# The first mixer's width-31 convolution as three of half the length, and a new order of the stage around it

## The chip, the core and the metric

The kernel runs on one core of a Trainium2 chip. The metric is the time of one execution on the device in microseconds (us), the median of several runs. PE is the matrix engine (TensorE), DVE the vector engine, ACT the scalar engine, POOL the GpSimd engine, SP the queue engine that issues most DMAs.

## What is computed

Four residual layers on 1024 frames of 1024 channels: a pool-and-convolution mixer, a gated FFN, a spatial gating unit and a second gated FFN, each behind an RMS norm. The change is in the first mixer alone:

```python
def pool_conv_mixer(h, w_in, pool_w, pool_scale, conv_w, conv_b, cn_g, cn_b, w_out):
    z = h @ w_in
    za = z[..., :D_POOL]
    zb_val = z[..., D_POOL:D_POOL + D_CONV]
    zb_gate = z[..., D_POOL + D_CONV:]
    pa = multiscale_pool_residual(za.reshape(bsz, s, POOL_GROUPS, POOL_GW))   # windows 2, 4, 8, 16: trailing mean minus za
    ya = jnp.einsum("bsgc,gcd->bsgd", pa, pool_w).reshape(bsz, s, D_POOL) * pool_scale
    gl = zb_val * jax.nn.sigmoid(zb_gate)
    yb = jax.nn.silu(layer_norm(causal_dwconv(gl, conv_w, conv_b), cn_g, cn_b))   # 31 taps per channel
    return jnp.concatenate([ya, yb], axis=-1) @ w_out
```

`D_POOL` and `D_CONV` are 512 each, so that there are four pool groups and four convolution blocks of 128 channels.

## The kernel before

Channels lie on the 128 partitions, frames along the free dimension, in two halves `h` of 512 frames (`HS`). Every fp32 product is made as three fp32r products of high and low parts (`mm3`, L185 to L189): a weight tile is loaded, ACT casts it to its high part `H` (L169), POOL subtracts to get the low part `L` (L170), and PE does H·H, H·L and L·H. A `gemm` of one 128-channel output block and both halves is 48 products of 512 columns. Weight tiles pass through few buffers (two raw, four for high and low parts), so a tile's cast waits for PE's last use of an earlier one.

The stage `mix0` runs, in PE's order: the value and gate of convolution block 0 (`gemm_pair`), with the norm of half 1 woven in (`n0`: the sums `st_n`, the root `r_n` on POOL, the broadcast `bc_n`; `have_rb` then makes `rb` and the first `glu`); value and gate of block 1; and then in turn the projections `za` of the four pool groups and the values and gates of blocks 2 and 3. Each `glu` makes `gl` = value × sigmoid(gate) in SBUF, with the norm's factor `rb` taken in (DVE L876 and L879, ACT L877, and L878 on POOL for blocks 1 to 3).

The convolution doesn't use PE. `conv(c, h, acc)` makes one half of one block: ACT starts `pc` in PSUM with one tap (L797), DVE adds taps one by one with a multiply-add over 512 frames (L807), and `NSIDE[c]` of the 31 taps go another way: ACT scales into `pr` (L801) and POOL adds (L805). DVE joins both sums (L812). The two halves of a block take turns (`convs`).

A pool group takes `u` from PSUM (DVE L899), forms its windowed sums by doubling on POOL (`s`, L904), and ends in `pa` on POOL (L911), once for each half. PE then mixes the group's channels (`ppool`, L916), and ACT and DVE split the result into `yaH` and `yaL` (L921, L922).

Behind that come `out_ya` (PE `poa`, 384 products), in which the layer norm `ln(0)` is woven (means `mb` of the four convolution outputs L936, sums `st_ln`, broadcast `bc_ln`, swish), then `out_yb` for each half (`pob`, 96 products each), with `ln(1)` in the first, and then the first FFN (`qa_u`).

PE's order is fixed by the program: it is the order of the code, with `later(n, fn)` hanging a step into a list that `tick` runs down by the count of 512-column products. The delays are the tables `LN0`, `LN1` and `N0LAG` and the arguments of `pool_group(g, delay)`. The other engines' orders are set when the program is built, by a scheduler that estimates when each instruction could start; the instructions of one engine then run in that order, each waiting for what it reads.

Of the kernel before, what the change touches and what calls it, by code (L numbers as in the profile page):

```python
# [10 lines left out]
F32 = mybir.dt.float32  # L11
# [3 lines left out]
ALU = mybir.AluOpType  # L15
# [13 lines left out]
PAD = 32  # L29

NSIDE = (9, 6, 8, 12)
# [4 lines left out]
LEAD = 6  # L36

LN0 = (36, 10, 4)
LN1 = (8, 10, 5)
WARM = 9  # L40
N0LAG = (20, 33)
# [28 lines left out]
def trunk_kernel(ctx: ExitStack, tc: tile.TileContext, a: dict, out: bass.AP):  # L70
# [708 lines left out]
    with stage("mix0", 8) as mp:  # L779
        pw = mp.tile([P, 4, P], F32, name="pw")  # L780
        gl = [mp.tile([P, PAD + S], F32, name=f"gl{c}") for c in range(4)]
        for c in range(4):
            nc.gpsimd.memset(gl[c][:, :PAD], 0.0)
        y = [[None, None] for _ in range(4)]

        def conv(c, h, acc):


            def src(k):
                o = PAD + h * HS - (CW - 1 - k)  # L790
                return gl[c][:, o : o + HS]

            def w(k):
                return col("conv_w", c * CW + k)

            n = f"{c}{h}"
            nc.scalar.activation(acc, src(CW - 1), AF.Identity, bias=col("conv_b", c), scale=w(CW - 1))  # L797
            side = None
            for k in range(NSIDE[c]):
                pr = mp.tile([P, HS], F32, tag="pr" if k else "side", name=f"pr{n}_{k}", bufs=2)  # L800
                nc.scalar.activation(pr, src(k), AF.Copy, scale=w(k))  # L801
                if side is None:
                    side = pr
                else:
                    nc.gpsimd.tensor_tensor(side, side, pr, op=ALU.add)  # L805
            for k in range(CW - 2, NSIDE[c] - 1, -1):
                yield nc.vector.scalar_tensor_tensor(acc, src(k), w(k), acc, op0=ALU.mult, op1=ALU.add)  # L807
            if h == 0:
                y[c][0] = mp.tile([P, HS], F32, tag="y", name=f"y{c}0", bufs=4)
            else:  # L810
                y[c][1] = gl[c][:, PAD + HS :]
            nc.vector.tensor_tensor(y[c][h], acc, side, op=ALU.add)  # L812

        def convs(a_, b_, lead=0):

            runs = [conv(*i, ps("pc%d%d" % i)) for i in (a_, b_)]
            for step in range(lead):
                ins = next(runs[0])
            with tc.issue_after(ins.ins) if lead else nullcontext():
                while runs:  # L820
                    runs = [r for r in runs if next(r, None) is not None]
# [384 lines left out]
```

## Time and profile before

| | us |
|---|---|
| median of 3 runs (1885.22 to 1887.01) | 1886.92 |
| the profiled execution | 1887.98 |
| its span in the trace | 1885.6 |
| from the start to the end of the last pool mix | 163.9 |
| from there to the first product of the first FFN (at 287.13) | 123.2 |

The granted clock of PE was 0.988 over the span. Times in the rows are microseconds from the start of the span unless marked ns. PE's matmuls are pipelined: a row's duration holds the modelled end of the last of them, and the step from one start to the next is what a product takes from the stream.

### The profile page before, as it was taken

Reading aid. Unit: us, or ns where it says so; the run is one execution under the profiler, and the core shown is the slowest. Engines: PE = TensorE matmul, PEld = TensorE weight load, DVE = VectorE, ACT = ScalarE, POOL = GpSimd, SP = SyncE. Lnnn points to the kernel's source line nnn. Section 1 sums busy time; section 2 is a strip of 40 time slices with the busy share of each in tenths; the row PEclk is TensorE's granted clock in tenths of the full one; section 3 lists DMA queues with packets and bytes.
Section 4 is the critical chain, followed back from the end, with each engine's and each line's share of the span. In section 5 each row is a group of like instructions: output and inputs, shape, how many; then the busy total and the mean of one; then the engine's idle time right before and its main releaser. Section 6 shows DMA issues by size and latency. Waiting matters only on the chain. (4 is left out here: it accounts for less than half of the span.)

```text
span 1885.6 us, 22755 instructions
## 1 busy us (share of the span) xinstructions
PE 1829.3 (97%) x8088; PEld 1501.4 (80%) x8092; DVE 1269.2 (67%) x1672; ACT 930.3 (49%) x1684; POOL 1238.9 (66%) x902
## 2 busy tenths in 40 slices
PE   8999888999999999999899999999999999999997
PEld 6787667888888888888778888777888888888886
DVE  5899788567676766886620247575767676768874
ACT  6436454655555565444431233356555555653461
POOL 2899667877777765685432445678777777656851
PEclk8999989999999999999999999999999999999998
DMA  4111121345444456542111222303444445565412
GB/s 157 45 46 34 54 92 34 115 131 168 145 146 156 149 175 233 185 134 79 43 48 56 90 89 101 100 23 123 155 147 163 150 146 167 168 234 167 141 56 89
DMA packets 113984, 223.26 MB, mean 118 GB/s; under 512 B 8784, under 2 KB 54864, under 8 KB 113872
## 3 DMA queue, kind: packets, MB, share of 16 engines
q1 hardware_dynamic: 113584, 221.55, 35.8%
q8 instruction: 63, 1.03, 0.2%
q14 instruction: 49, 0.40, 0.1%
q10 hardware_dynamic: 288, 0.28, 0.0%
HBM read 171.46 MB, written 50.33 MB: 118 GB/s over the span
## 5 line engine op out<-in xcount | busy, mean ns | idle before, releaser
L630 POOL TENSOR_TENSOR w<-d,w 128x512 fp32r<-128x512 f32 x154 | 232.1, 1527 | 124.0 <-ACT w L672 123.9
L357 POOL TENSOR_TENSOR w_u<-S_u,w_u 128x512 fp32r<-128x512 f32 x160 | 208.4, 1302 | 113.5 <-ACT w_u L356 113.5
L334 PE MATMUL p<-set,w 128*128 128x512 f32 x616 | 240.8, 391 | 3.6 <-DVE set L323 3.6
L333 PE MATMUL p<-set,w 128*128 128x512 f32 x616 | 240.9, 391 | 0.6 <-ACT set L322 0.6
L335 PE MATMUL p<-set,w 128*128 128x512 f32 x616 | 240.2, 390 | 0.0
L357 POOL TENSOR_TENSOR w_u<-r_u,w_u 128x512 fp32r<-128x512 f32 x120 | 156.6, 1305 | 59.5 <-ACT w_u L356 58.5
L333 PE MATMUL qb_u<-set,w_u 128*128 128x512 f32 x480 | 187.0, 389 | 0.1
L334 PE MATMUL qb_u<-set,w_u 128*128 128x512 f32 x480 | 186.7, 389 | 0.0
L335 PE MATMUL qb_u<-set,w_u 128*128 128x512 f32 x480 | 186.7, 389 | 0.0
L322 ACT CAST set<-hid 128x512 fp32r<-128x512 f32 x154 | 90.8, 620 | 162.6 <-DVE hid L630 97.4
L323 DVE TENSOR_TENSOR set<-hid,set 128x512 fp32r<-128x512 f32 x132 | 129.9, 1015 | 55.3 <-ACT set L322 52.9
L559 DVE SCALAR_TENSOR_TENSOR z<-qb_u,cols,z 128x511 f32<-128x511 f32 x88 | 65.9, 749 | 140.6 <-ACT z L557 139.1
L356 ACT CAST w_u<-S_u 128x512 fp32r<-128x512 f32 x160 | 98.7, 617 | 93.8 <-PE qb_u L335 60.8
L334 PEld LDWEIGHTS p<-set,w 128*128 128x128 f32 x616 | 116.0, 188 | 29.3 <-DVE set L323 5.3
L333 PEld LDWEIGHTS p<-set,w 128*128 128x128 f32 x616 | 115.9, 188 | 25.3 <-ACT set L322 1.0
L335 PEld LDWEIGHTS p<-set,w 128*128 128x128 f32 x616 | 116.1, 188 | 23.8
L335 PE MATMUL qa_u<-set,w_u 128*128 128x512 f32 x320 | 124.6, 389 | 0.6 <-POOL w_u L357 0.6
L333 PE MATMUL qa_u<-set,w_u 128*128 128x512 f32 x320 | 124.6, 389 | 0.2 <-ACT w_u L356 0.2
L334 PE MATMUL qa_u<-set,w_u 128*128 128x512 f32 x320 | 124.5, 389 | 0.0
L333 PE MATMUL qe_u<-set,w_u 128*128 128x512 f32 x320 | 124.5, 389 | 0.0
L334 PE MATMUL qe_u<-set,w_u 128*128 128x512 f32 x320 | 124.5, 389 | 0.0
L335 PE MATMUL qe_u<-set,w_u 128*128 128x512 f32 x320 | 124.5, 389 | 0.0
(241 smaller groups left out, 4772.0 us busy)
## 6 DMA issues: line engine op xcount, KB each, us to landing
r_u<-in_w_up SPq DMA_DIRECT2D x88, 512.0 KB, 3.4
hid<-z SPq DMA_DIRECT2D x44, 512.0 KB, 3.1
ws<-in_w_down SPq DMA_DIRECT2D x88, 256.0 KB, 3.6
sums<-ws SPq DMA_DIRECT2D x88, 256.0 KB, 3.7
hid<-hid SPq DMA_DIRECT2D x44, 512.0 KB, 5.6
d<-sums SPq DMA_DIRECT2D x40, 512.0 KB, 4.3
d<-in_w_down SPq DMA_DIRECT2D x30, 512.0 KB, 4.0
r_wv<-in_od_in SPq DMA_DIRECT2D x16, 512.0 KB, 3.8
```

The lines of the kernel that those rows point to most:

```text
L322: nc.scalar.copy(t[:, 0], src)
L323: leng.tensor_tensor(t[:, 1], src, t[:, 0].bitcast(F32), op=ALU.subtract)
L333: nc.tensor.matmul(o, H, xH, start=first, stop=False, skip_group_check=True)
L334: nc.tensor.matmul(o, H, xL, start=False, stop=False, skip_group_check=True)
L335: nc.tensor.matmul(o, L, xH, start=False, stop=last, skip_group_check=True)
L356: nc.scalar.copy(H, src)
L357: nc.gpsimd.tensor_tensor(L, src, H.bitcast(F32), op=ALU.subtract)
L559: nc.vector.scalar_tensor_tensor(o[:, s:], src[:, : HS - s], w[2 - s], o[:, s:], op0=ALU.mult, op1=ALU.add)
L630: eng.tensor_tensor(o, one, two, op=op)
```

## The change

- A block's convolution is split by even and odd frames. `gl` is stored de-interleaved, `xe` and `xo` of 512 each behind a pad of 16 (`CT`), and POOL adds `xs` = `xe` + `xo` over 528 elements, from both halves of the frames at once. Three convolutions of length 512 follow: `e` of `xe` with the 16 even taps, `o` of `xo` with the 15 odd ones, and one of `xs` with the 16 sums of neighbouring taps. Even outputs are `e` plus `o` shifted by one, odd ones are the third minus `e` and `o`. Results are written over `gl` with a step of two elements.
- Per block there are then 45 or 46 taps over 512 elements where there were 62. `NSIDE` of the 16 summed taps go by ACT and POOL: (9, 9, 11, 14), once per block, where (9, 6, 8, 12) went there for each half. `tap_sums` makes the summed taps and twice the bias on DVE, right behind the load of `cols`.
- `glu` reads its PSUM operands and `rb` with a step of two and writes de-interleaved.
- `val_gate(3)` stands ahead of `conv(2)` and the pool groups 1 and 0, and `conv(3)` ahead of `pool_group(0)`. The lead of the last convolution (`LEAD`, `convs`) goes.
- `ln(1)` is hung in before `out_ya`, with a delay of 54 products in place of 8 behind it. The norm's lags become 42 (from 33) and 7 (from 3). The buffers of `rb` are their own.

```diff
@@ -26,19 +26,18 @@
 DFF = 2816
 NF = DFF // P
 NB = 2
-PAD = 32
-
-NSIDE = (9, 6, 8, 12)
+
+CT = (CW + 1) // 2
+
+NSIDE = (9, 9, 11, 14)
 
 BUFS = {"wr": 2, "wh": 4}
 FFN_BUFS = {"hl": 4, "raw": 2, "z": 3}
 
-LEAD = 6
-
 LN0 = (36, 10, 4)
-LN1 = (8, 10, 5)
+LN1 = (54, 10, 5)
 WARM = 9
-N0LAG = (20, 33)
+N0LAG = (20, 42)
 NORM_LAG = ((8, 10), (6, 5))
 
 SUM_TWICE = (4, 8, 12, 16)
@@ -778,52 +777,76 @@
 
     with stage("mix0", 8) as mp:
         pw = mp.tile([P, 4, P], F32, name="pw")
-        gl = [mp.tile([P, PAD + S], F32, name=f"gl{c}") for c in range(4)]
+
+        gl_flat = [mp.tile([P, 2 * CT + S], F32, name=f"gl{c}") for c in range(4)]
+        gl = [g.rearrange("p (r n) -> p r n", r=2) for g in gl_flat]
         for c in range(4):
-            nc.gpsimd.memset(gl[c][:, :PAD], 0.0)
-        y = [[None, None] for _ in range(4)]
-
-        def conv(c, h, acc):
-
-
-            def src(k):
-                o = PAD + h * HS - (CW - 1 - k)
-                return gl[c][:, o : o + HS]
+            nc.gpsimd.memset(gl[c][:, :, :CT], 0.0)
+        y = [[g[:, 2 * CT + h * HS : 2 * CT + (h + 1) * HS] for h in range(2)] for g in gl_flat]
+        wsum = mp.tile([P, 4, CT], F32, name="wsum")
+        bias2 = mp.tile([P, 4], F32, name="bias2")
+
+        def tap_sums():
+
+            c0 = COLS["conv_w"]
+            w = cols[:, c0 : c0 + 4 * CW].rearrange("p (c k) -> p c k", k=CW)
+            nc.vector.tensor_copy(wsum[:, :, :1], w[:, :, :1])
+            nc.vector.tensor_tensor(wsum[:, :, 1:], w[:, :, 1::2], w[:, :, 2::2], op=ALU.add)
+            b0 = COLS["conv_b"]
+            nc.vector.tensor_tensor(bias2, cols[:, b0 : b0 + 4], cols[:, b0 : b0 + 4], op=ALU.add)
+
+
+
+
+
+        def conv(c):
+            xe, xo = [gl[c][:, r] for r in range(2)]
+            xs = mp.tile([P, CT + HS], F32, tag="xs", name=f"xs{c}", bufs=2)
+            nc.gpsimd.tensor_tensor(xs, xe, xo, op=ALU.add)
+            b = col("conv_b", c)
 
             def w(k):
                 return col("conv_w", c * CW + k)
 
-            n = f"{c}{h}"
-            nc.scalar.activation(acc, src(CW - 1), AF.Identity, bias=col("conv_b", c), scale=w(CW - 1))
+            def late(src, d):
+                return src[:, CT - d : CT - d + HS]
+
+            e, o = [ps(f"pc{i}{c}") for i in "eo"]
+            nc.scalar.activation(e, late(xe, 0), AF.Identity, bias=b, scale=w(CW - 1))
+            nc.scalar.activation(o, late(xo, 0), AF.Copy, scale=w(CW - 2))
             side = None
             for k in range(NSIDE[c]):
-                pr = mp.tile([P, HS], F32, tag="pr" if k else "side", name=f"pr{n}_{k}", bufs=2)
-                nc.scalar.activation(pr, src(k), AF.Copy, scale=w(k))
+                pr = mp.tile([P, HS], F32, tag="pr" if k else "side", name=f"pr{c}_{k}", bufs=2)
+                ws = wsum[:, c, k : k + 1]
                 if side is None:
+                    nc.scalar.activation(pr, late(xs, CT - 1 - k), AF.Identity, bias=bias2[:, c : c + 1], scale=ws)
                     side = pr
                 else:
+                    nc.scalar.activation(pr, late(xs, CT - 1 - k), AF.Copy, scale=ws)
                     nc.gpsimd.tensor_tensor(side, side, pr, op=ALU.add)
-            for k in range(CW - 2, NSIDE[c] - 1, -1):
-                yield nc.vector.scalar_tensor_tensor(acc, src(k), w(k), acc, op0=ALU.mult, op1=ALU.add)
-            if h == 0:
-                y[c][0] = mp.tile([P, HS], F32, tag="y", name=f"y{c}0", bufs=4)
-            else:
-                y[c][1] = gl[c][:, PAD + HS :]
-            nc.vector.tensor_tensor(y[c][h], acc, side, op=ALU.add)
-
-        def convs(a_, b_, lead=0):
-
-            runs = [conv(*i, ps("pc%d%d" % i)) for i in (a_, b_)]
-            for step in range(lead):
-                ins = next(runs[0])
-            with tc.issue_after(ins.ins) if lead else nullcontext():
-                while runs:
-                    runs = [r for r in runs if next(r, None) is not None]
+
+            def add(acc, src, d, wt):
+                nc.vector.scalar_tensor_tensor(acc, late(src, d), wt, acc, op0=ALU.mult, op1=ALU.add)
+
+            for d in range(1, CT):
+                add(e, xe, d, w(CW - 1 - 2 * d))
+                if d < CT - 1:
+                    add(o, xo, d, w(CW - 2 - 2 * d))
+            yr = gl_flat[c][:, 2 * CT :].rearrange("p (n r) -> p n r", r=2)
+            nc.scalar.copy(yr[:, :1, 0], e[:, :1])
+
+            os = npool.tile([P, HS], F32, tag="acc", name=f"os{c}")
+            nc.scalar.copy(os, o)
+            nc.vector.tensor_tensor(yr[:, 1:, 0], e[:, 1:], os[:, : HS - 1], op=ALU.add)
+            nc.vector.scalar_tensor_tensor(e, e, -1.0, os, op0=ALU.mult, op1=ALU.subtract)
+            for k in range(CT - 1, NSIDE[c] - 1, -1):
+                add(e, xs, CT - 1 - k, wsum[:, c, k : k + 1])
+            nc.vector.tensor_tensor(yr[:, :, 1], e, side, op=ALU.add)
 
 
         n0 = [Norm("mix_g", 0, "n0"), Norm("mix_g", 0, "n0", mp, ("side", "pr"))]
         h0 = new_act(KT)
-        rb = [mp.tile([P, HS], F32, tag="y", name=f"rb{h}", bufs=4) for h in range(2)]
+        rb = [mp.tile([P, HS], F32, name=f"rb{h}") for h in range(2)]
 
         warm = ps("warm")
         for i in range(WARM):
@@ -847,6 +870,7 @@
                 for k in range(KT):
                     nc.sync.dma_start(x[k][:, half(1)], xT[k * P : (k + 1) * P, half(1)])
         nc.scalar.dma_start(cols, cols_d)
+        tap_sums()
         nc.sync.dma_start(pw, a["pool_w"].rearrange("g c d -> c g d"))
         for h in range(2):
             for k in range(KT):
@@ -865,18 +889,19 @@
             with tc.issue_after((made if h else last_split).ins):
                 for k in range(KT):
                     n0[h].feed(k, h, nc.gpsimd if k % 2 and not h else nc.vector)
-            n0[h].apply(h, have_rb, N0LAG[h], 3)
+            n0[h].apply(h, have_rb, N0LAG[h], 7)
 
         def w_in(f):
             return wtile(a["ev_in"][f], f"win{f}")
 
         def glu(c, pv, pg):
             for h in range(2):
-                g = gl[c][:, PAD + h * HS : PAD + (h + 1) * HS]
-                nc.vector.tensor_tensor(g, pg[h], rb[h], op=ALU.mult)
+                g = gl[c][:, :, CT + h * HS // 2 : CT + (h + 1) * HS // 2]
+                pvh, pgh, r = [t.rearrange("p (n r) -> p r n", r=2) for t in (pv[h], pg[h], rb[h])]
+                nc.vector.tensor_tensor(g, pgh, r, op=ALU.mult)
                 nc.scalar.activation(g, g, AF.Sigmoid)
-                (nc.gpsimd if c else nc.vector).tensor_tensor(g, g, rb[h], op=ALU.mult)
-                nc.vector.tensor_tensor(g, pv[h], g, op=ALU.mult)
+                (nc.gpsimd if c else nc.vector).tensor_tensor(g, g, r, op=ALU.mult)
+                nc.vector.tensor_tensor(g, pvh, g, op=ALU.mult)
 
         def val_gate(c):
             pv, pg = [gemm(w_in(f), h0, f"vg{f}") for f in (4 + c, 8 + c)]
@@ -997,20 +1022,20 @@
 
         p0 += gemm_pair(first, h0, "vg0")
         val_gate(1)
-        convs((0, 0), (0, 1))
+        conv(0)
         pool_group(3, 40)
         val_gate(2)
-        convs((1, 0), (1, 1))
+        conv(1)
         pool_group(2, 40)
-        convs((2, 0), (2, 1))
+        val_gate(3)
+        conv(2)
         pool_group(1, 40)
+        conv(3)
         pool_group(0, 31)
-        val_gate(3)
-        convs((3, 0), (3, 1), LEAD)
         tick(1000)
         ln(0, LN0)
+        ln(1, LN1)
         out_ya()
-        ln(1, LN1)
         out_yb(0)
         out_yb(1)
```

How the rows move at three places, rows in an engine's order. **POOL, around `pa` of group 3** (`pr` are the side sums of a convolution, `s` and `pa` the pool group, `L_win` a weight's low part). Before:

```order
L904 TENSOR_TENSOR s_8_712<-s_4_710 128x512
L908 TENSOR_TENSOR s_8_712<-s_8_712,inv_cnt 128x16
L904 TENSOR_TENSOR s_1_720<-u_717 128x526
L911 TENSOR_TENSOR pa_702<-s_8_712,u_703 128x512
L170 TENSOR_TENSOR L_win_942<-r_win_939,H_win_941 128x1024
L904 TENSOR_TENSOR s_2_722<-s_1_720 128x524
L805 TENSOR_TENSOR pr_0_853<-pr_0_853,pr_1_855 128x512
L904 TENSOR_TENSOR s_4_724<-s_2_722 128x520
L805 TENSOR_TENSOR pr_0_853<-pr_0_853,pr_2_858 128x512
L904 TENSOR_TENSOR s_8_726<-s_4_724 128x512
L805 TENSOR_TENSOR pr_0_853<-pr_0_853,pr_3_861 128x512
L911 TENSOR_TENSOR pa_702<-s_8_726,u_717 128x512
```

Now:

```order
L169 TENSOR_TENSOR L_win_995<-r_win_992,H_win_994 128x1024
L933 TENSOR_TENSOR s_8_690<-s_8_690,inv_cnt 128x16
...
L903 TENSOR_TENSOR gl_130<-gl_130,rb_138 128x2x256
L903 TENSOR_TENSOR gl_130<-gl_130,rb_139 128x2x256
L936 TENSOR_TENSOR pa_680<-s_8_690,u_681 128x512
...
L805 TENSOR_TENSOR xs_1112<-gl_130 128x528
L929 TENSOR_TENSOR s_4_702<-s_2_700 128x520
L929 TENSOR_TENSOR s_8_704<-s_4_702 128x512
L826 TENSOR_TENSOR pr_0_1118<-pr_0_1118,pr_1_1120 128x512
L936 TENSOR_TENSOR pa_680<-s_8_704,u_695 128x512
L826 TENSOR_TENSOR pr_0_1118<-pr_0_1118,pr_2_1123 128x512
```

Before, the 16 side sums of block 0 stood ahead of the rows shown, and three of block 1's between them. Now all eight of block 0 and all eight of block 1 stand ahead of them, with both their `xs`; and the `gl` and `xs` of block 2 and its first side sum stand ahead of the second half's `pa`.

**The last two pool mixes**: on POOL, from the low part `L_win` of the last tile of the stage, before and now:

```order
L170 TENSOR_TENSOR L_win_1343<-r_win_1340,H_win_1342 128x1024
L911 TENSOR_TENSOR pa_1182<-s_2_1188,u_1183 128x512
...
L911 TENSOR_TENSOR pa_1182<-s_2_1198,u_1193 128x512
L908 TENSOR_TENSOR s_1_1262<-s_1_1262,inv_cnt 128x2
L904 TENSOR_TENSOR s_1_1270<-u_1267 128x512
L911 TENSOR_TENSOR pa_1258<-s_1_1262,u_1259 128x512
L911 TENSOR_TENSOR pa_1258<-s_1_1270,u_1267 128x512
L805 TENSOR_TENSOR pr_0_1032<-pr_0_1032,pr_1_1034 128x512
```
```order
L169 TENSOR_TENSOR L_win_1363<-r_win_1360,H_win_1362 128x1024
L903 TENSOR_TENSOR gl_131<-gl_131,rb_138 128x2x256
...
L805 TENSOR_TENSOR xs_1276<-gl_131 128x528
L826 TENSOR_TENSOR pr_0_1282<-pr_0_1282,pr_1_1284 128x512
...
L936 TENSOR_TENSOR pa_1256<-s_2_1262,u_1257 128x512
...
L936 TENSOR_TENSOR pa_1256<-s_2_1272,u_1267 128x512
L826 TENSOR_TENSOR pr_0_1282<-pr_0_1282,pr_9_1308 128x512
...
L929 TENSOR_TENSOR s_1_1428<-u_1425 128x512
L826 TENSOR_TENSOR pr_0_1282<-pr_0_1282,pr_13_1320 128x512
L936 TENSOR_TENSOR pa_1416<-s_1_1420,u_1417 128x512
L936 TENSOR_TENSOR pa_1416<-s_1_1428,u_1425 128x512
```

On PE before, and now:

```order
L189 MATMUL p_vg_1_1347<-act_223,L_win_1343 128x512
L916 MATMUL ppool_0_1372<-pa_1182,pw 128x512
L916 MATMUL ppool_1_1373<-pa_1182,pw 128x512
L186 MATMUL p_vg_0_1346<-act_202,H_win_1342 128x512
...
L189 MATMUL p_vg_1_1347<-act_235,L_win_1343 128x512
L916 MATMUL ppool_0_1406<-pa_1258,pw 128x512
L916 MATMUL ppool_1_1407<-pa_1258,pw 128x512
L186 MATMUL poa_0_1543<-yaH_975,H_evoa_1539 128x512
```
```order
L188 MATMUL p_za_0_1366<-act_216,L_win_1363 128x512
L188 MATMUL p_za_1_1367<-act_240,L_win_1363 128x512
L941 MATMUL ppool_0_1432<-pa_1256,pw 128x512
L941 MATMUL ppool_1_1433<-pa_1256,pw 128x512
L941 MATMUL ppool_0_1442<-pa_1416,pw 128x512
L941 MATMUL ppool_1_1443<-pa_1416,pw 128x512
L185 MATMUL poa_0_1458<-yaH_938,H_evoa_1454 128x512
```

On POOL, the side sums of blocks 2 and 3 stood behind the last `pa`; now all of them stand ahead of it. On PE, the mixes of groups 1 and 0 stood with 24 products of block 3's gate between them; now the gate has gone ahead, and both mixes stand together in front of `poa`.

**PE, the mean of the second half.** Before, and now:

```order
L187 MATMUL pob_1869<-act_1796,H_evob_1849 128x512
L189 MATMUL pob_1869<-act_1796,L_evob_1850 128x512
L936 MATMUL mb_1882<-gl_128,mean_c 128x512
L936 MATMUL mb_1882<-gl_129,mean_c 128x512
L936 MATMUL mb_1882<-gl_130,mean_c 128x512
L936 MATMUL mb_1882<-gl_131,mean_c 128x512
L186 MATMUL pob_1912<-act_1775,H_evob_1908 128x512
```
```order
L188 MATMUL poa_0_1673<-yaH_1436,L_evoa_1670 128x512
L188 MATMUL poa_1_1674<-yaH_1436,L_evoa_1670 128x512
L961 MATMUL mb_1726<-gl_128,mean_c 128x512
L961 MATMUL mb_1726<-gl_129,mean_c 128x512
L961 MATMUL mb_1726<-gl_130,mean_c 128x512
L961 MATMUL mb_1726<-gl_131,mean_c 128x512
L185 MATMUL poa_0_1673<-yaH_1446,H_evoa_1669 128x512
```

It stood in the first half's `pob`, 24 products in; it now stands in `poa`, 30 products before its end.

## Rows read from the trace of the kernel before

**Rows 1.** The page, part 1: busy time, share of the span and instructions.
```profile
PE 1829.3 (97%) x8088; PEld 1501.4 (80%) x8092; DVE 1269.2 (67%) x1672; ACT 930.3 (49%) x1684; POOL 1238.9 (66%) x902
```

**Rows 2.** Windows: span, then PE, PEld, DVE, ACT, POOL busy; clock, DMA, GB/s.
```profile
61.00:107.64 46.64, 46.64 (x207) 38.63 (x206) 44.74 (x70) 17.95 (x25) 39.66 (x30) 1.00 0.14 46
107.64:163.90 56.26, 56.26 (x233) 43.30 (x231) 55.50 (x89) 25.64 (x37) 51.82 (x45) 1.00 0.15 47
163.90:287.13 123.23, 108.06 (x450) 84.47 (x449) 100.38 (x137) 61.83 (x94) 86.72 (x56) 0.93 0.21 65
```

**Rows 3.** Waits of PE, 0 to 350 us: in all, times, longest.
```profile
PE pob L187 <- DVE act L170: 5.2, 2, 2.7
...
PE poa L186 <- DVE yaL L922: 2.1, 2, 1.4
PE pob L189 <- POOL L_evob L170: 1.6, 1, 1.6
PE st_ln L217 <- DVE lacc L945: 1.5, 1, 1.5
```

**Rows 4.** Timeline of PE: start, us, instruction, idle before.
```profile
44.14 0.94 PE L217 MATMUL st_n<-ones,sq_n 128*128 128x1 f32 x8
...
50.82 1.16 PE L237 MATMUL bc_n<-ident,r_n 128*128 128x128 f32 x8 [2.85 <-POOL r_n L229]
...
69.56 0.39 PE L186 MATMUL p_za<-act,H_win 128*128 128x512 f32 x1
...
107.64 1.88 PE L916 MATMUL ppool<-pa,pw 128*128 128x512 f32 x4
...
162.04 1.88 PE L916 MATMUL ppool<-pa,pw 128*128 128x512 f32 x4
...
198.43 2.08 PE L936 MATMUL mb<-y,mean_c 128*128 128x512 f32 x2 [4.81 <-DVE y L812]
...
229.50 3.59 PE L936 MATMUL mb<-gl,mean_c 128*128 128x512 f32 x8
232.53 0.80 PE L186 MATMUL pob<-act,H_evob 128*128 128x512 f32 x1
...
239.77 0.95 PE L217 MATMUL st_ln<-ones,lacc 128*128 128x1 f32 x8
...
287.13 0.39 PE L333 MATMUL qa_u<-set,we_u 128*128 128x512 f32 x1
```

**Rows 5.** Groups of POOL by line, 40 to 210 us: busy, mean ns; idle.
```profile
L805 POOL TENSOR_TENSOR pr<-pr,pr 128x512 f32<-128x512 f32 x62 | 80.9, 1307 | 6.8 <-ACT pr L801 3.8
L170 POOL TENSOR_TENSOR L_win<-r_win,H_win 128x1024 fp32r<-128x1024 f32 x10 | 24.1, 2407 | 13.9 <-ACT H_win L169 13.8
...
L904 POOL TENSOR_TENSOR s<-s 128x512 f32<-128x512 f32 (+3 forms) x12 | 13.1, 1094 | 0.5
L911 POOL TENSOR_TENSOR pa<-s,u 128x512 f32<-128x512 f32 x8 | 10.4, 1302 | 0.0
...
L904 POOL TENSOR_TENSOR s<-u 128x526 f32<-128x526 f32 (+3 forms) x8 | 8.4, 1051 | 0.2
L878 POOL TENSOR_TENSOR gl<-gl,rb 128x512 f32<-128x512 f32 x6 | 7.8, 1304 | 0.0
```

**Rows 6.** Timeline of POOL: first convolution adds, `pa` of groups 3 and 0.
```profile
43.56 2.66 POOL L805 TENSOR_TENSOR pr<-pr,pr 128x512 f32<-128x512 f32 x2 [2.72 <-ACT pr L801]
...
101.62 1.34 POOL L911 TENSOR_TENSOR pa<-s,u 128x512 f32<-128x512 f32 x1
...
145.73 2.56 POOL L911 TENSOR_TENSOR pa<-s,u 128x512 f32<-128x512 f32 x2
```

**Rows 7.** Timeline of DVE: the first convolution's multiply-adds.
```profile
56.29 13.27 DVE L807 SCALAR_TENSOR_TENSOR pc<-gl,cols,pc 128x512 f32<-128x512 f32 x20 [0.26 <-ACT pc L797]
```

**Rows 8.** Groups of ACT by line, 40 to 210 us: busy, mean ns; idle.
```profile
L801 ACT ACTIVATE pr<-gl,cols 128x512 f32<-128x512 f32 x70 | 49.4, 720 | 47.4 <-POOL pr L805 39.4 <-DVE gl L879 7.8
...
L169 ACT CAST H_win<-r_win 128x1024 fp32r<-128x1024 f32 x9 | 9.4, 1048 | 12.8 <-PE p_za L187 9.9 <-PE p_vg L187 2.9
```

## The prediction, made before the changed kernel ran

> **What bounds the kernel now.** The page's first part comes first: TensorE (PE) is busy for 97% of the span, so the program is a stream of products with few holes, and only an edit that fills or opens a hole in PE's stream moves the time [rows 1]. The windows of the first mixer show where the holes are. From PE's third pool projection to the end of the last pool mix PE is full, with the granted clock at 1.00; in the 123.23 us from there to the first product of the FFN it is busy for 108.06, at a clock of 0.93 [rows 2]. The waits of PE name what ends those holes: `yaL` (2.1 us), the convolution's result `y` ahead of the mean (4.81), `lacc` (1.5), `act` ahead of the second half's `pob` (5.2), a weight's low part (1.6), and earlier `r_n` (2.85) [rows 3, 4]. POOL is busy for 51.82 of the 56.26 us before the last pool mix, hidden so far: its `pa` of group 3 starts at 101.62 and PE asks for it at 107.64; its last `pa` starts at 145.73 (two of 1.28) and PE asks at 162.04 [rows 2, 4, 6].
>
> Times below are positions in the profiled execution: 1887.98 us, 1.06 above the median 1886.92.
>
> **The change part by part.**
>
> *Fewer passes.* DVE's convolution goes from 178 passes to 149, 137 of them multiply-adds: 29 × 0.66 (20 back to back in 13.27) is 19 us less [rows 7]. ACT's scalings go from 78 to 55, at 0.72 each [rows 8]. POOL's adds go from 62 to 39 plus four `xs`: 19 × 1.3 is 25 us less [rows 5]. PE's products are the same in number. These gains are worth only what PE's waits get back, so the rest is about when things are done. The three operations on DVE for `wsum` and `bias2`, the eight copies on ACT for `os` and the first output, and DVE's strided operands I cost at nothing: POOL's work, below, covers them, since DVE's 149 passes of about 0.66 and some 25 others like them are 115 us, which from 61 on are done near 178, before POOL. Without that cover each strided pass of DVE could cost up to another 0.66.
>
> *First norm's lag.* `st_n` of half 1 moves 24 products back in PE's order and `bc_n` now stands 24 products behind it. One product is (107.64 − 69.56)/168 = 0.227 us [rows 4]. So `st_n` is at 44.14 + 5.4 = 49.6 and `bc_n`, 0.8 + 5.4 later, at 55.8 in place of 50.82. PE's wait of 2.85 for `r_n` goes, since POOL is no longer behind convolution adds there; group 3's projection starts at 66.7, not 69.56. But what hangs on `bc_n` is 5 us later: the first convolution's multiply-adds began 5.5 after it, at 56.29, and now begin near 61.3 [rows 4, 7].
>
> *POOL's first stretch.* Before, half 0 could be convolved alone, and POOL's adds began at 43.56 [rows 6]. `xs` needs both halves, so now none begins before about 61. In POOL's new order there stand ahead of the second half of `pa` of group 3, from 61 on: 17 convolution adds (22.2), four low parts of weights at 2.41 (9.6), four `gl` products at 1.30 (5.2), group 3's eight `s` at 1.09, a small one and two `pa` (11.5) and three `xs` [rows 5]. `xs` is not in the trace. The nearest rows are `s<-u` of the same width, 1.05, and `pr`, 1.31 [rows 5]; both add two fp32 operands, and I take 1.2 between them (3.6). That is 52.1, and with some 2.4 us of gaps `pa` is ready at 115.5. PE, without a wait, is at the mix at 66.7 + 168 × 0.227 = 104.8. **PE waits some 10 us** (in two pieces, for the two halves), and the mix ends near 116.5. Other work queued behind it on PE is the value and gate of block 3: all later by that.
>
> *POOL's second stretch.* Gate 3 is now ahead of the second and third pool mix. From the mix, 120 products (27.2) and 1.5 for a lower clock after the wait bring PE to the end of gate 3 at 145.2. Only then is its weight buffer free: ACT's cast (1.05) and POOL's low part follow, then `gl` of block 3 (2 × 1.30), DVE's last factor, `xs`, and ACT's first scalings (four of 0.72 to 0.77), so that the third convolution's adds begin near 157 [rows 5, 8]. POOL idles for some 4 us before that. In its order between there and the last `pa`: 13 adds (16.9), two low parts (4.8), six `s` (6.4), four `pa` (5.2) and two small ones, 33 us: **pa of group 0 is ready near 190.2**. PE has nothing but 96 products and one mix left after gate 3; it is at the mixes of groups 1 and 0, which now stand back to back, at 168.9. It waits some 20 us in pieces; the last mix ends at 191.1. Before it ended at 163.9 [rows 4]: **27.2 us later**.
>
> *What is won behind it.* From the end of the mixes to the FFN's first product were 287.13 − 163.9 = 123.2 us [rows 4]. There are 384 products (87.0), two means of 3.0 (the step from 229.50 to 232.53), and six small groups of `st` and `bc` of about 0.85: 98.1 without holes. Now the convolutions are all done when the mixes end, so `y` (4.81) and `yaL` (2.1) are there in time; the second half's layer norm stands early, its mean ahead of 30 products of `poa`, and its swish has 81 products where it had 27 ahead of its `pob`, so `act` (5.2) goes too; the clock that fell after these waits stays up. I keep the 1.5 for `lacc`, the 1.55 for a low part, and 1.6 for one fall of the clock: 102.8. **20.4 us are won.** Were the two waits for POOL shorter, `y` of block 3, which DVE finishes near 188, would be late next, ahead of the first mean.
>
> *Strided operands on POOL.* `gl *= rb` now reads and writes `gl` de-interleaved and reads `rb` with a step of two elements. No row shows a step on POOL. Bounds: nothing, or twice the row's 1.30, which is 4 × 1.3 = 5.2 in the first stretch and 2.6 in the second [rows 5]. I take nothing, since the nearest row, with a step of one, is all the trace has; the other end stays for the range. The Trainium skill ("GPSIMD Engine Reference", Performance pitfalls for Q7 kernels) states a cost of half as much again, but only for reads whose inner step is above 8 bytes; the step here is 8, so that by it the term would be nothing, which no row so far shows or denies.
>
> *Sum:* + 27.2 − 20.4 = + 6.8 on the FFN's first product; all behind it is unchanged. 1887.98 + 6.8 is 1894.8 in the profiled execution, and **1894** against the median.
>
> **The rivals.**
>
> *No change that can be told.* A measurement of this kernel can tell about 0.2%, 3.8 us, from nothing. POOL's 30 adds in the two stretches take 1.1 us in place of 1.31, near the `s` row's 1.05 [rows 5]: the last `pa` comes 6 us earlier, the sum is + 1, and the time 1888. For it: both rows add fp32 operands of some 512 elements. Against it: 62 such adds average 1.307, of two different tiles as here, while `s<-u` adds a tile to itself, shifted. The Trainium skill ("GPSIMD Engine Reference", Performance versus the Vector engine) gives 4497 ns for a two-input add of 2048 fp32 elements; a quarter of it, an estimate, is 1.12 us. By it this rival would be the forecast; the measured 1.307 of the same operation is what I go by.
>
> *Faster.* The mechanism is the same chain of POOL, at the lowest price that the rows allow: every add and `xs` at the 1.05 of `s<-u`, with no gap between them. Its place is PE's last pool mix, and the point from which it decides is 180.5: there the 20.4 won behind it outweigh the delay by 3.8. 30 × 0.26, 4 × 0.15 and the 2.4 of gaps are 10.8, which puts the end of the mixes at 180.3 and the time at 1883; each further us on POOL is another won. For it: POOL has 25 us of adds less in all, so little has to come free. Against it: most of those that went stood behind the pool mixes, where no one waited for them, and the adds' row is an average over 62. With no wait at all at the mixes all of the 20 us would be won (1867); that needs a POOL 27 us faster, and gets almost no chance.
>
> *Slower still.* The step doubles `gl *= rb` on POOL (5.2 + 2.6 = 7.8 more on the chain): 1902; with the granted clock low for longer after the two waits, up to 1904.
>
> *The change doesn't do what it says*: the order on POOL is set when the program is built, and the rows of it are fixed; no chance of its own.
>
> **How the numbers follow.** The forecast, slower by 4 to 12 us, gets 0.52; slower still 0.13; no change 0.19; faster 0.16. The range reaches from 1883, the short end of POOL's prices, to 1904, the step doubled and a longer fall of the clock: about 0.1 lies below, 0.08 above. The likeliest case alone is 1891 to 1899. Slower by over 0.2%: 0.65; within: 0.19; faster: 0.16.
>
> **What would show it.** In the changed profile, PE's waits should have `ppool` behind POOL's `pa`: near 10 us between 104 and 117, near 20 us between 169 and 191. The waits for `y` and `r_n` should be gone, and those for `act` with `pob`. POOL should be busy without a pause from 61 to 141, then idle some 4 us for ACT's `H_win`. The stretch from the last mix to the first `qa_u` should be near 103 us. The prediction is wrong if the waits at `ppool` add up to less than 20, or if that stretch stays above 115; a `gl` product on POOL well above 1.3 us would put it in the upper part of the range.

## The result, and the profile after

The changed kernel takes 1900.74 us in the median of four runs (1899.47 to 1903.22), beside 1886.95 for the kernel before in the same comparison: a ratio of 1.0078, 95% interval 1.0066 to 1.009. It is slower by 13.8 us; the forecast was slower by 7, in a range (1883 to 1904) that holds the result. The likeliest case, 1891 to 1899, does not hold it: 13.8 lies beyond the 4 to 12 us that had the chance of 0.52, in the case "slower still" (0.13). The profiled execution took 1901.43 us, with a span of 1899.5.

First the page's part 1 of the changed kernel, busy time and share by engine, which answers to [rows 1].

```profile
PE 1831.0 (96%) x8088; PEld 1501.3 (79%) x8092; DVE 1247.0 (66%) x1646; ACT 915.1 (48%) x1665; POOL 1211.2 (64%) x883
```

Every engine but PE has less to do (DVE 1247.0 for 1269.2, POOL 1211.2 for 1238.9), and PE has the same; what grew is PE's idle time. The waits of PE up to 360 us name it (total, times, longest), and answer to [rows 3].

```profile
PE ppool L941 <- POOL pa L936: 18.6, 4, 7.8
PE st_n L216 <- DVE sq_n L260: 12.8, 3, 4.9
PE ppool L941 <- DVE pce L829: 5.9, 1, 5.9
```

The waits of [rows 3, 4], for `yaL`, `y`, `lacc`, `act`, `L_evob` and `r_n`, are all gone. In their place PE waits 24.5 us at the pool mixes (the 5.87 put down to DVE's `pce` ends at 178.17, and POOL's `pa` of that half at 178.12, in a row below), and at `st_n` for 12.8, of which 4.79 stand at the first norm (5.34 before). The timeline of PE (start, length, instruction, idle time before it and its releaser) shows where, as [rows 4] did.

```profile
56.49 1.05 PE L236 MATMUL bc_n<-ident,r_n 128*128 128x128 f32 x8
...
66.94 0.39 PE L185 MATMUL p_za<-act,H_win 128*128 128x512 f32 x1
...
107.88 1.18 PE L941 MATMUL ppool<-pa,pw 128*128 128x512 f32 x2 [2.29 <-POOL pa L936]
115.51 2.07 PE L941 MATMUL ppool<-pa,pw 128*128 128x512 f32 x2 [6.45 <-POOL pa L936]
...
171.18 1.12 PE L941 MATMUL ppool<-pa,pw 128*128 128x512 f32 x2 [2.08 <-POOL pa L936]
178.17 2.08 PE L941 MATMUL ppool<-pa,pw 128*128 128x512 f32 x2 [5.87 <-DVE pce L829]
188.01 3.78 PE L941 MATMUL ppool<-pa,pw 128*128 128x512 f32 x4 [7.76 <-POOL pa L936]
190.80 1.42 PE L185 MATMUL poa<-yaH,H_evoa 128*128 128x512 f32 x1
...
276.64 1.86 PE L216 MATMUL st_n<-ones,sq_n 128*128 128x1 f32 x8 [4.89 <-DVE sq_n L260]
278.37 0.78 PE L185 MATMUL pob<-act,H_evob 128*128 128x512 f32 x1
...
283.30 1.05 PE L236 MATMUL bc_n<-ident,r_n 128*128 128x128 f32 x8
...
300.56 0.39 PE L332 MATMUL qa_u<-set,we_u 128*128 128x512 f32 x1
...
308.16 1.05 PE L216 MATMUL st_n<-ones,sq_n 128*128 128x1 f32 x8 [3.10 <-DVE sq_n L260]
```

`poa` starts at 190.80, where it started at 165.33 before. From the end of the mixes to the first product of the FFN there were 123.2 us and are 300.56 − 190.80 = 109.8, so that 13.4 come back. (The 163.9 before is the modelled end of the last mix and the 190.80 the start of `poa` behind it; from `poa` to `poa` it would be 12.0.) At that product the program is 13.4 behind. The next half's `st_n` waits 3.10 for its squares, where it waited 0.59, and behind it the program is 16.3 behind. Of that 2.3 come back near the end of the program, where PE's clock was low in the profile before (0.51 of full from 1840.9 to 1844.4) and isn't in the one after; the spans differ by 13.9.

POOL's timeline is the chain that PE waits for.

```profile
61.09 1.33 POOL L805 TENSOR_TENSOR xs<-gl 128x528 f32<-128x528 f32 x1 [2.66 <-DVE gl L904]
63.96 4.05 POOL L826 TENSOR_TENSOR pr<-pr,pr 128x512 f32<-128x512 f32 x3 [1.54 <-ACT pr L825]
...
114.16 1.29 POOL L936 TENSOR_TENSOR pa<-s,u 128x512 f32<-128x512 f32 x1
...
146.34 2.40 POOL L169 TENSOR_TENSOR L_win<-r_win,H_win 128x1024 fp32r<-128x1024 f32 x1 [4.37 <-ACT H_win L168]
...
156.71 1.29 POOL L826 TENSOR_TENSOR pr<-pr,pr 128x512 f32<-128x512 f32 x1 [2.65 <-ACT pr L825]
...
176.85 1.27 POOL L936 TENSOR_TENSOR pa<-s,u 128x512 f32<-128x512 f32 x1
...
186.67 2.51 POOL L936 TENSOR_TENSOR pa<-s,u 128x512 f32<-128x512 f32 x2
```

POOL begins the first convolution at 61.09 (it was 43.56 in [rows 6]), ends `pa` of group 3 at 115.45 (102.96 before), then waits 4.37 us for ACT's high part of the weight behind gate 3, and ends the last `pa` at 189.18 (148.29 before). The groups of POOL by line (count, busy, mean ns, idle) answer to [rows 5].

```profile
L826 POOL TENSOR_TENSOR pr<-pr,pr 128x512 f32<-128x512 f32 x39 | 50.1, 1286 | 5.2 <-ACT pr L825 4.2
...
L903 POOL TENSOR_TENSOR gl<-gl,rb 128x512 f32<-128x512 f32 x6 | 7.7, 1303 | 0.0
...
L805 POOL TENSOR_TENSOR xs<-gl 128x528 f32<-128x528 f32 x4 | 5.3, 1322 | 4.5 <-DVE gl L904 4.5
```

The new `xs` costs 1.32, like any add of the side sums (1.29), and the product with the strided `rb` 1.303, what it cost without a step (1.304).

### The profile page after: what moved, and what is told of

It is laid out like the page before. It is cut to its first block, busy times and chain, and to the rows that moved or that the text cites. A ratio compares the mean times of both kernels' runs of the same rounds, so it can differ in the third digit from the quotient of the medians.

```text
span 1899.5 us, 22666 instructions
## 1 busy us (share of the span) xinstructions
PE 1831.0 (96%) x8088; PEld 1501.3 (79%) x8092; DVE 1247.0 (66%) x1646; ACT 915.1 (48%) x1665; POOL 1211.2 (64%) x883
## 3 DMA queue, kind: packets, MB, share of 16 engines
q8 instruction: 63, 1.03, 0.2%
## 5 line engine op out<-in xcount | busy, mean ns | idle before, releaser
L629 POOL TENSOR_TENSOR w<-d,w 128x512 fp32r<-128x512 f32 x154 | 231.2, 1520 | 123.2 <-ACT w L671 121.9
```

The costliest lines, as they stand in the source:

```text
L629: eng.tensor_tensor(o, one, two, op=op)
```

## The experiments

The theory: PE's order asks for `pa` at the old places, while POOL's order now has the convolutions' side sums ahead of `pa`; that is the loss of some 25 us, and the earlier layer norm and the shorter convolution win half of it back. Rivals: the new form of the convolution is the cost, or DVE, or what stands behind the mixes.

### The pool groups first again

```diff
         pool_group(2, 40)
-        val_gate(3)
         conv(2)
         pool_group(1, 40)
-        conv(3)
         pool_group(0, 31)
+        val_gate(3)
+        conv(3)
```

> The changed kernel with one thing undone: pool groups 1 and 0 stand ahead of value and gate 3, and the third convolution last, as before the change; the new convolution, the early layer norm and the lags stay. Theory (POOL's convolution work ahead of pa is what holds PE): PE's wait at the mix of group 3 stays at some 8.7 us, those at the mixes of groups 1 and 0 (15.7 us) go, poa starts near 171 in place of 190.8, and the third convolution, now late, costs a wait of some 2 to 4 us at the first mean: 1881 to 1886. Rival (the new form of the convolution is itself the cost, by its strided operands and its sums over both halves): the time stays above 1895.

Measured: 1892.02 us, ratio to the kernel before 1.0035 (1.0023 to 1.0047). PE's timeline:

```profile
113.67 2.08 PE L941 MATMUL ppool<-pa,pw 128*128 128x512 f32 x2 [5.83 <-POOL pa L936]
...
169.92 0.79 PE L185 MATMUL poa<-yaH,H_evoa 128*128 128x512 f32 x1
...
203.81 2.05 PE L961 MATMUL mb<-gl,mean_c 128*128 128x512 f32 x2 [5.39 <-DVE gl L844]
...
290.74 0.80 PE L332 MATMUL qa_u<-set,we_u 128*128 128x512 f32 x1 [2.98 <-DVE x L1019]
```

The waits at the last two mixes are gone, that at the mix of group 3 stays (8.1 in all), and `poa` starts at 169.92, as the theory had it. But the whole is won only in part: gate 3 is now last on PE, the third convolution can't start before it, and PE waits 5.39 for its output at the first mean, where I had allowed 2 to 4, and 3 us more ahead of the FFN. The time lies between the two theories' ranges; the start of `poa` decides for the order, and the rest is a second price, of a convolution that needs the whole block before it begins.

### Fewer side sums

```diff
-NSIDE = (9, 9, 11, 14)
+NSIDE = (6, 6, 7, 8)
```

> The changed kernel with NSIDE (6, 6, 7, 8) in place of (9, 9, 11, 14): 16 adds fewer on POOL (21 us), 16 multiply-adds more on DVE (11 us). Theory (POOL's chain holds PE): pa of group 3 comes 9 us earlier, so that PE's wait there is under 2 us, pa of group 0 near 172, poa starts near 174, and the time is 1881 to 1888. Rival (DVE's convolution, or a bank of PSUM that it holds, is the late one at the mixes): the waits at the mixes stay or grow by the 11 us, and the time is 1900 or more.

Measured: 1899.41 us, ratio 1.0076 (1.0061 to 1.0091): nothing won. The wait at the mix of group 3 falls from 8.74 to 3.24 (I had under 2). Those at the last two mixes don't fall: 18.6 in all, for 15.7. POOL's row of the last `pa`, and ACT's rows ahead of it:

```profile
180.92 1.29 POOL L936 TENSOR_TENSOR pa<-s,u 128x512 f32<-128x512 f32 x1 [9.28 <-ACT s L935]
```

```profile
179.42 0.59 ACT L839 COPY os<-pco 128x512 f32<-128x512 f32 x1 [10.54 <-DVE pco L829]
...
180.15 0.63 ACT L935 ACTIVATE s<-s 128x510 f32<-128x510 f32 x1
```

POOL is idle for 9.28 us, waiting for ACT's scaling of `s`; ACT runs its list in order, and ahead of that scaling stands the copy `os` of the third convolution, for which ACT waits 10.54 us on DVE's `pco`. So the rival is right here in its cause, if 0.6 us short of its time: with 16 multiply-adds moved to DVE, DVE becomes the late one, and reaches the pool group through ACT's queue. In the changed kernel both are late at once: DVE starts on the result of block 3, the last of the convolutions, at 187.11, POOL on the last `pa` at 186.67.

### The early layer norm, taken back and alone

```diff
-LN1 = (54, 10, 5)
+LN1 = (8, 10, 5)
...
-        ln(1, LN1)
         out_ya()
+        ln(1, LN1)
```

> The changed kernel with the second half's layer norm back behind out_ya, delay 8. Theory (the early norm gains the wait for act but opens the one for sq_n at the FFN's norm, so that little is left): the wait for sq_n (4.9) goes, those for act come back (about 5), poa still starts near 190.8, and the time is within 3 us of the changed kernel's 1900.7. Rival (the early norm is what won the 13 us behind the mixes): 1908 or more.

The reverse of it in the kernel before:

> The kernel before with one part of the change alone: the second half's layer norm ahead of out_ya with a delay of 54. Theory: the waits for act (5.2) go and a wait of some 5 for sq_n ahead of the FFN's norm takes their place: 1884 to 1888. Rival (the norm alone is worth the waits for act and the low clock behind them, some 8 us): 1880 or less.

Measured: 1903.88 us (1.0098; 1.0083 to 1.0113) without it in the changed kernel, and 1887.04 (0.9999; 0.9978 to 1.002) with it alone in the kernel before. Waits of PE in both, the first two rows without it, the others with it alone:

```profile
PE pob L186 <- DVE act L169: 5.8, 2, 3.3
...
PE pob L188 <- POOL L_evob L169: 1.5, 1, 1.5
```

```profile
PE st_n L217 <- DVE sq_n L261: 4.7, 1, 4.7
PE qa_u L333 <- DVE x L994: 3.1, 1, 3.1
```

The early norm takes the 5 to 6 us for `act` away and puts 4.7 for `sq_n` and 3.1 ahead of the FFN in their place. In the kernel before that is worth nothing that can be told; in the changed one some 3 us (the expectation said within 3, it is 3.1; the two runs were not compared with each other, and the intervals of their ratios to the kernel before overlap). So it isn't what won the 13 us. The waits for `y` and `yaL` stay away without the early norm too, since the convolutions are done when the mixes end.

### The mix of group 3 later

```diff
-        pool_group(3, 40)
+        pool_group(3, 56)
```

> The changed kernel with the mix of pool group 3 hung 48 products later (delay 56 in place of 40), nothing else. Theory (the end of the mixes is set by one chain of POOL work): PE's wait of 8.7 us at that mix goes, but the pause of POOL at 142 (4.4 us, for the weight behind gate 3) is all that the chain has to give, so pa of group 0 comes some 4 us earlier, the wait turns up at the last mixes, poa starts near 186, and the time is 1895 to 1898. Rival (the two waits are independent costs): the whole wait and its low clock go, 10 us, poa starts near 181 and the time is 1889 to 1892.

Measured: 1894.67 us (1.0046; 1.0031 to 1.0062). PE's timeline:

```profile
116.71 1.12 PE L941 MATMUL ppool<-pa,pw 128*128 128x512 f32 x2 [0.65 <-POOL pa L936]
...
182.28 1.42 PE L185 MATMUL poa<-yaH,H_evoa 128*128 128x512 f32 x1
...
297.38 0.80 PE L332 MATMUL qa_u<-set,we_u 128*128 128x512 f32 x1 [5.14 <-DVE x L1019]
```

Here my theory of one rigid chain fell: `poa` starts 8.5 us earlier, nearly the whole wait. (Of these, 1.3 stand already at the first product of group 3's projection, 65.66 for 66.94, ahead of anything that was edited; 7.2 are the edit's, between the 4.4 of the theory and the 10 of the rival, as the time is.) The chain ran over PE. POOL's pause at 142 was a wait for PE's gate 3, and PE was late there because it had waited for POOL at 115; with PE on time POOL has its weight at once, and its order (built anew) has no pause over 2.1 us between 107 and 179. Its pauses from 107 to the last `pa` add up to 3.2 us, where they were 9.6: not only the 4.4 went, but most of what POOL waited behind it for DVE's `gl` and ACT's first `pr` as well. At the FFN's first product, which now waits 5.14 for DVE's last `x`, only 3.2 of the 8.5 are left; 3.1 come back at the next half's `st_n`, which waits no longer, and the time is 6.1 us less.

### The norm's sums later

```diff
-            n1.apply(h, to_h1, *((4, 4), NORM_LAG[1])[h])
+            n1.apply(h, to_h1, *((12, 4), NORM_LAG[1])[h])
```

> The changed kernel with the sums of the FFN's first norm 24 products later (lag 12 in place of 4), nothing else. Theory (the early layer norm left PE without cover for the last squares, which DVE finishes 2.5 to 5 us after the last product of the half): the wait for sq_n (4.9) and the low clock behind it (some 2 us) go, none takes their place, and the time is 1893 to 1896. Rival (the squares are late because DVE's order is full, and what hangs on the norm is late next): a wait of 3 us or more ahead of the first products of the FFN, and a time within 3 us of 1900.7.

Measured: 1899.85 us (1.0072; 1.0056 to 1.0087). The rival holds in the time: `sq_n` no longer makes PE wait at this norm, and two other waits take its place, the larger of them for a weight's low part on POOL, which neither theory named:

```profile
PE pob L188 <- POOL L_evob L169: 4.0, 1, 4.0
PE qa_u L333 <- DVE set L322: 2.4, 1, 2.4
```

### Gate 3 between the last two pool groups

```diff
-        pool_group(3, 40)
+        pool_group(3, 56)
...
-        val_gate(3)
         conv(2)
         pool_group(1, 40)
-        conv(3)
+        val_gate(3)
         pool_group(0, 31)
+        conv(3)
```

> A version that could beat both: the changed kernel with the mix of group 3 at delay 56, the second convolution's and pool group 1's order as before the change, and value and gate 3 between the pool groups 1 and 0, the third convolution last. Theory: pa of group 0 has only five side sums of the third convolution ahead of it on POOL, PE's waits at the mixes are under 5 us in all, poa starts at 163 to 169, the third convolution is done by 190, before the first mean, and the time is 1874 to 1880. Rival (as in the order with gate 3 last: the third convolution is late at the first mean): a wait of 5 us there, and 1885 or more.

> The last version and the norm's lag of 12 together. Theory: the two gains add, since they lie on both sides of poa: 5 to 7 us less than the version without the lag, 1868 to 1875. Rival: the lag gives back what it gains ahead of the FFN, and the time is within 3 us of that version.

Measured: 1895.43 us (1.0053; 1.004 to 1.0065), and with the lag of 12 as well 1893.63 (1.004; 1.0027 to 1.0053). Both miss their theories; of the second the rival holds (1.8 us less, within its 3). PE's timeline of the first:

```profile
131.68 0.80 PE L185 MATMUL p_vg<-act,H_win 128*128 128x512 f32 x1 [8.38 <-DVE yaL L947]
...
180.21 3.78 PE L941 MATMUL ppool<-pa,pw 128*128 128x512 f32 x4 [9.87 <-POOL pa L936]
```

Neither theory named the first of these waits: value 3's first product into its second half waits 8.38 us for `yaL`, which DVE makes from the mix of group 3 at 130.88, behind multiply-adds. What the product needs of `yaL` is no data; that it writes the PSUM bank that `yaL` reads is the only link that I see, but it was not tested apart. With 8.4 us lost there, the third convolution and the last projection come together again, and PE waits 9.87 for `pa`.

### The side sums of block 3 behind the last pa

```diff
+                    with tc.issue_after(after.ins) if after else nullcontext():
-                    nc.gpsimd.tensor_tensor(side, side, pr, op=ALU.add)
+                        nc.gpsimd.tensor_tensor(side, side, pr, op=ALU.add)
...
-        conv(3)
-        pool_group(0, 31)
+        conv(3, pool_group(0, 31))
```

`pool_group` returns its last `pa`, and POOL's 13 sums of block 3 are put behind it in POOL's order; in the code the convolution now follows pool group 0.

> The changed kernel with one thing moved: the third convolution's 13 side sums on POOL stand behind the last pa, and that convolution behind pool group 0 in the code. Theory (these 13 sums, 17 us, ahead of pa of groups 1 and 0 are what holds PE at the last mixes): the wait of 8.7 us at the mix of group 3 stays, those at the mixes of groups 1 and 0 fall from 15.7 to 3 to 5 us (what u, s and pa take behind the last projection), poa starts near 175 in place of 190.8, the third convolution is done before the first mean at 200, and the time is 1884 to 1891, the spread being a wait of up to 5 us at the first product of the FFN, as in the run with the later mix. Rival (DVE, through ACT's copies, is as late as POOL, as with fewer side sums): pa of group 0 still waits for ACT, poa starts after 183, and the time is 1893 or more.

With the later mix of group 3 as well:

> The last version with the mix of group 3 hung 48 products later as well. Theory (both waits of PE are POOL's, and with both gone the shorter convolution leaves the gains behind the mixes): no wait over 5 us up to poa, which starts at 164 to 169; the waits for sq_n (5) and at the first product of the FFN (5) stay; 1877 to 1883, under both kernels. Rival (what is won at the mixes is given back behind them, by the third convolution at the first mean or the norm of the FFN): poa as early, but 1885 or more.

Measured: 1888.67 us for the first, ratio 1.0006 (0.9994 to 1.0019), no change from the kernel before; and **1880.75 us for both, ratio 0.9962 (0.9949 to 0.9975), faster than either kernel**. PE's timeline, the first two rows of the first version, the others of the second:

```profile
175.02 3.78 PE L942 MATMUL ppool<-pa,pw 128*128 128x512 f32 x4 [4.89 <-POOL pa L937]
177.82 1.42 PE L185 MATMUL poa<-yaH,H_evoa 128*128 128x512 f32 x1
```

```profile
163.90 1.13 PE L942 MATMUL ppool<-pa,pw 128*128 128x512 f32 x2 [1.68 <-POOL pa L937]
...
169.71 3.78 PE L942 MATMUL ppool<-pa,pw 128*128 128x512 f32 x4 [4.68 <-DVE pco L830]
172.50 1.42 PE L185 MATMUL poa<-yaH,H_evoa 128*128 128x512 f32 x1
...
284.10 0.80 PE L332 MATMUL qa_u<-set,we_u 128*128 128x512 f32 x1 [3.07 <-DVE x L1021]
```

and POOL's last `pa` in the second version:

```profile
168.38 2.52 POOL L937 TENSOR_TENSOR pa<-s,u 128x512 f32<-128x512 f32 x2
```

Moving 13 sums of POOL behind the last `pa`, with the convolution behind that pool group in the code, is worth 12 us; the two were not tried apart. Of the 4.89 that stay, about half is POOL's low part of a weight of `poa` (169.12, 2.36), which stands ahead of `s`. `poa` starts at 177.82, 13.0 earlier (I had 175), and the third convolution is still done near 197 on DVE, before the first mean at 203.6. With the other wait gone as well, `poa` starts at 172.50; the last mix still costs 4.68, what `u`, `s` and `pa` take behind the last projection (the row puts the wait down to `pco`, but the first of the two `pa` ends at the same time). So `poa` is later than the 164 to 169 expected, and the time is inside what the theory gave and well under its rival. Of the 5.6 us won against the kernel before, 2.7 stand already at the first product of group 3's projection (66.88 for 69.56), ahead of the mixes, where PE no longer waits for `r_n`; whether the first norm's later lag alone would give them in the kernel before was not tried.

## Why the prediction was right, point by point

- *What bounds the kernel, and that fewer passes are worth only PE's waits*: right. DVE's 22 us and POOL's 28 us less bought nothing by themselves. Two counts were off and enter no sum: a block has 47 taps over 512 elements (16, 15 and 16), not 45 or 46, and ACT's scalings go to 51 (8 first taps and 43 of `NSIDE`), not 55.
- *First norm's lag*: `bc_n` at 56.49 (forecast 55.8), group 3's projection at 66.94 (66.7), `xs` at 61.09 (61).
- *POOL's first stretch*: `pa` ready at 115.45 (115.5), PE's wait 8.74 in two pieces (10). `xs` costs 1.32, not 1.2.
- *POOL's second stretch*: pause 4.37 (4), first add at 156.71 (157), last `pa` at 189.18 (190.2), waits 15.7 in three pieces (20), end of the mixes at 190.80 (191.1). So 26.9 us later, for 27.2. That this is so close is in part luck: the waits are 24.5 us where the sum had some 30, and PE's granted clock, for which it had 1.5, was at 0.50 (1.2 GHz) from 108.8 to 119.1 and from 173.7 to 194.2, while PE waited and behind it, which cost some 5 (an estimate: the 123.9 us from group 3's projection to `poa`, less the waits and the 94.3 that the same work took before). The runs that moved the side sums and the mix show the mechanism; what they add is that the two waits feed each other over gate 3, which my sum had in it as the pause, and that DVE, whose passes I had done near 178, starts the last at 187.11, so that it is as late as POOL: from 61 on it has 31 passes besides the 149, not 25, and stands idle for 11 us, 4.92 of them for gate 3 on PE. So POOL's work covered DVE's only just, where the term had it done 12 us sooner; DVE's strided passes cost nothing all the same (`gl`, 683 ns on average, 687 before).
- *Strided operands on POOL*: nothing, as taken: 1.303 us beside 1.304. The Trainium skill ("GPSIMD Engine Reference", Performance pitfalls for Q7 kernels) states an extra cost only for a step above 8 bytes; the trace agrees with it at 8.
- *The price of POOL's adds*: 1.29 for the side sums and 1.32 for `xs`, which decides against the rivals of no change and of faster. The quarter of the Trainium skill's figure ("GPSIMD Engine Reference", Performance versus the Vector engine), an estimate of 1.12, is too low for these adds; the measurement decides.
- *What is won behind it*: this is the term that was mis-sized, 20.4 forecast and 13.4 measured, and it is the 7 us between forecast and result. The waits for `y`, `yaL` and `act` went as said, and even `lacc` and the low part, which I had kept (3 us). The step that failed is that nothing would be late next but `y` of block 3. Late was `sq_n`: the last square of the half stands on ACT behind four casts of weights, its sum ends on DVE at 276.6, and PE waits 4.89 (`st_n`, above). The clock is then low (0.50 from 276.1 to 282.9): the twelve products from 278.37 to 283.30 take 4.9 us where 2.7 would do at full clock, and where they took 4.75 before, behind the wait for `act`. The 1.6 kept for a fall of the clock went on the first products of `poa`, before 194.2. Before, the waits for `act` had slowed the products ahead of `st_n` and so hidden the squares; with the early norm taken back those waits return and that `st_n` waits for nothing. That all behind the FFN's first product is unchanged came out by luck too: 2.9 more are lost at the next `st_n`, and 2.3 come back at the end.

The timelines of ACT, of DVE and of POOL in the changed kernel show that chain:

```profile
271.63 1.66 ACT L355 CAST we_u<-r_u 128x512 fp32r<-128x512 f32 x3 [1.07 <-DMA r_u<-in_w_up]
273.19 1.04 ACT L168 CAST H_evob<-r_evob 128x1024 fp32r<-128x1024 f32 x1
274.14 0.62 ACT L258 ACTIVATE sq_n<-x 128x512 f32<-128x512 f32 x1
```

```profile
274.80 1.79 DVE L260 TENSOR_TENSOR sq_n<-sq_n,sq_n 128x512 f32<-128x512 f32 x1 [2.41 <-ACT sq_n L258]
```

```profile
272.32 3.71 POOL L356 TENSOR_TENSOR we_u<-r_u,we_u 128x512 fp32r<-128x512 f32 x3 [1.08 <-ACT we_u L355]
```

DVE's last sum takes 1.79 us there. Such a sum of two tiles in SBUF takes 0.69 where POOL is idle (from 265.73 in this trace); here, and in the four others of this half that take longer, it ends some 0.55 us after an instruction of POOL has ended (276.03, the row above). So some 1.1 us of PE's 4.89 are DVE held up by POOL.

- *The slower rival* gave a time near the result (1902) for another reason, the step doubling `gl *= rb`. It didn't happen. The upper end of the range was set by it, so that the range holds the result by luck.

What stays open: why the first product of the FFN waits for DVE's last `x` in some of these versions (5.14 with the later mix alone, 3.07 with the side sums moved too) and not in the changed kernel; where it waits for `x`, the next half's `st_n` (3.10 in the changed kernel) does not. Which PSUM bank it takes over may differ with the build, but that was not tested. And whether the old convolution, put into the best order found here, would do as well as the new one was not tried.

## What to carry to other kernels

Less work on an engine won nothing here until the order was looked at: find the few results that the bounding engine asks for (`pa` here), and count what stands ahead of each in its producer's order, after the change as well as before. A scheduler that goes by when an instruction could start can put work that nobody waits for ahead of them; moving it behind (13 sums and their convolution) won 12 us. And where a wait goes, add up the chain behind the next thing that is asked for, since the old wait may have been its cover (here `sq_n`, 4.89 us).

## What was not expected

- A wait of POOL for PE and one of PE for POOL were one loop: taking PE's 8.7 us away moved `poa` by 7.2 from group 3's projection on, not by the 4.4 that POOL paused.
- An in-order queue joins chains that share no data: with fewer side sums POOL idled 9.28 us for a scaling of 0.63 on ACT, which stood behind a copy that waited 10.54 on DVE.
- `xs` adds the two halves of one tile at 1.32 us, `s<-u` a tile to itself, shifted, at 1.05; so it isn't having one tile as both operands that makes `s` cheap. How far the shift goes does matter: a tile added to itself shifted by 1, 2 or 4 elements takes 1.03 to 1.08 us in every trace of this case, shifted by 8 (the last doubling of group 3) 1.28 to 1.32. In the changed kernel, shifts by 4 and by 8:

```profile
95.45 1.07 POOL L929 TENSOR_TENSOR s<-s 128x520 f32<-128x520 f32 x1
...
97.71 1.32 POOL L929 TENSOR_TENSOR s<-s 128x512 f32<-128x512 f32 x1
```

Why is open. The mean of `s` in [rows 5], 1.094, mixes the two.
